# S5 recurrence over chunks: a tree in place of a step-by-step scan

## The chip, the core and the metric

The kernel runs on one core of one Trainium2 chip. TensorE multiplies matrices, VectorE (DVE in the rows) and ScalarE (ACT) work elementwise, GpSimd (POOL) does some elementwise work, memsets and DMA issues, and SyncE (SP) issues most DMAs. The metric is the device time of one execution in microseconds (us), the median of several.

## The reference

One layer of a hybrid decoder for 512 prompt tokens and 8 x 4 sample tokens. The part that matters here is the S5 mixer, a complex recurrence with a diagonal matrix, in 64 groups of 64 states:

```
bu = einsum('btgc,gpc->btgp', u, B)        # complex, as real and imaginary arrays
x_t = lam * x_(t-1) + bu_t                 # per group and state
y = real(einsum('btgp,gcp->btgc', x, C)) + d * u
y = gelu(y);  y = y * sigmoid(y @ glu_w + glu_b)
```

Beside it stand the projections of the normed input (f, q, i, g for eight HGRN2 heads, u for the S5 mixer), the HGRN2 recurrence, an output projection and an MLP with 8192 hidden columns. The final S5 state is an output too.

## The kernel before

All values are float32. To keep the precision, each weight and each activation is split into a high and a low part, and a product is three matmuls (high x high, high x low, low x high). `weights` (L203) loads half of a unit's weights (`wf`, eight 128x128 blocks, three buffers), rounds them on ScalarE to `wh` (L210) and takes the low part `wl = wf - wh` (L211) on the engine that `state["lo"]` names: VectorE at first, GpSimd from gate 1 on, VectorE again after the first S5 outputs. `wh` and `wl` have two buffers. `unit` (L220) makes 128 columns of a projection from two such halves, 96 matmuls over 544 tokens. The units run in this order: u0 to u7, gates g0 to g7, then f, q, i of head 0, of head 1, and so on. A gate (L533) scales the product on VectorE (`gp`), takes a tanh on ScalarE and multiplies on VectorE.

The S5 recurrence is done over chunks of L = 4 tokens. `chunk_inputs(b)` (L563) lets TensorE sum each chunk's inputs (`px`) with maps that `input_maps(b)` (L551) builds on VectorE (`MB`) and transposes (`pw`); ScalarE copies the sums into `XX`, a tile of 128 partitions x 2 (real, imaginary) x 32 pairs of groups x 137 slots, one slot for each chunk: 8 sample slots, a zero slot, then 128 prompt chunks. Two groups of 64 states share the 128 partitions, so one of the 32 `NPR` entries is a pair of groups. Then x_j = lam^4 x_(j-1) + XX_j runs over the 128 prompt slots. In before this is `scan_steps` (L611): for each step j, six VectorE instructions on one slot (two halves of 16 pairs; each one multiply by `coef`, which holds lam^4, and two adds). 13 steps are written behind each of g1 to g7 and behind f, q, i of head 0, and `tc.manual_schedule` fixes the order on VectorE as it is written. Everywhere else a scheduler sets the order of each engine at build time; `tc.high_priority` lifts the weights and the scaling.

After the scan: the final state (`fin`, L641, transposed by TensorE, `pf`), then for each block b of eight pairs' outputs `output_maps(b)` (`CL`, `pk`) and `outputs(b)` (`py`, which reads XX), interleaved with head 1's f, q, i; then the heads, output projection, MLP.

Of the kernel before, what the change touches and what calls it, by code (L numbers as in the profile page):

```python
# [9 lines left out]
F32 = mybir.dt.float32  # L10
# [11 lines left out]
SEQ = 512  # L22
# [18 lines left out]
def trunk_kernel(  # L41
# [66 lines left out]
    with tc.high_priority():  # L108
# [133 lines left out]
    with pool("xs") as xp, tc.manual_schedule(engines={ENG.PE, ENG.Activation, ENG.DVE}):  # L242
# [14 lines left out]
        for k in range(KD + LAG):  # L257
            if k in (1, 8):
                w0[k // 8] = weights(None, 8, P, f"u0_{k}", w_first[k // 8])
            if k < KD:  # L260
                g, e = k // 4, k % 4
# [8 lines left out]
                hi, lo = h_acts[k]  # L270
# [12 lines left out]
            if k >= LAG:  # L283
                j = k - LAG
# [25 lines left out]
    with pool("mk") as mk:  # L310
# [28 lines left out]
    hga = hga_cm.__enter__()  # L339
# [3 lines left out]
    XX = s5.tile([P, 2, NPR, NSLOT], F32, name="XX")  # L343
# [4 lines left out]
    coef = s5.tile([P, 2, 2, NPR], F32, name="coef")  # L348
# [216 lines left out]
    def chunk_inputs(b, WB, ush):  # L565
        for q in range(4):
            i = 4 * b + q
            px = bank(f"px{i}")
            for r in range(2):
                T.matmul(px[:, r * NJ:(r + 1) * NJ], WB[r][:, q, :], ush[:, q, :], start=True, stop=True)  # L570
            pxv = px[:, :2 * NJ].rearrange("p (r j) -> p r j", r=2)
            A.copy(XX[:, :, i, NB + 1:], pxv[:, :, NB:])
            A.copy(WS[:, :, i, :], pxv[:, :, :NB])

    maps = {}
    for n, (mb, ib) in enumerate((([0, 1], []), ([2], [0, 1]), ([3], [2]), ([4], [3]), ([5, 6], [4]), ([7], [5]), ([], [6, 7])), 2):
# [12 lines left out]
    def project(h, after):

        pf = unit(W_IN, FC + P * h, h_acts, f"f{h}")
        f, k, q, v = (hga.tile([P, NT], F32, tag=t, name=f"{t}{h}") for t in "fkqv")
        scaled(f, pf)
        A.activation(f, f, AF.Tanh, scale=0.5)
        V.tensor_scalar(f, f, lbA[:, h:h + 1], lbB[:, h:h + 1], op0=ALU.mult, op1=ALU.add)
        V.tensor_scalar(k, f, -1.0, 1.0, op0=ALU.mult, op1=ALU.add)
        after(0)
        pq = unit(W_IN, QC + P * h, h_acts, f"q{h}")
        scaled(q, pq)
        A.activation(v, q, AF.Tanh, scale=0.5)  # L600
        V.scalar_tensor_tensor(q, v, 1.0, q, op0=ALU.add, op1=ALU.mult)
        after(1)
        pv = unit(W_IN, IC + P * h, h_acts, f"i{h}")
        scaled(v, pv)
        after(2)
        heads[h] = (f, k, q, v)


    s5c_cm = pool("s5c", 2, side="right")
    s5c = s5c_cm.__enter__()  # L610
    HPR = NPR // 2  # L611

    def scan_steps(j0, j1):
        for j in range(j0, min(j1, SEQ // L)):
            part = []
            for g in range(2):
                gs = slice(g * HPR, g * HPR + HPR)
                t = s5c.tile([P, 2, 2, HPR], F32, tag=f"sc{g}", name=f"sc{g}_{j}")
                part.append((t, XX[:, :, gs, NB + j], XX[:, :, gs, NB + 1 + j], coef[:, :, :, gs]))
            for t, xj, xn, cf in part:  # L620
                V.tensor_tensor(t, cf, xj[:, None].to_broadcast([P, 2, 2, HPR]), op=ALU.mult)
            for t, xj, xn, cf in part:
                V.tensor_tensor(xn, xn, t[:, 0], op=ALU.add)
            for t, xj, xn, cf in part:
                V.tensor_tensor(xn, xn, t[:, 1, ::-1, :], op=ALU.add)

    STEPS = 13
    state["lo"] = G
    with tc.manual_schedule(engines={mybir.EngineType.DVE}):
        for k in range(1, 8):  # L630
            gate(k, hga)
            scan_steps(STEPS * (k - 1), STEPS * k)
        project(0, lambda j: scan_steps(STEPS * (7 + j), SEQ // L if j == 2 else STEPS * (8 + j)))
    for a in range(2):
        t = s5c.tile([P, 2, NPR, NB], F32, tag="yn", name=f"scs{a}")
        V.tensor_tensor(t, coef[:, a, :, :, None].to_broadcast([P, 2, NPR, NB]), XX[:, :, :, 0:NB], op=ALU.mult)
# [268 lines left out]
    for k in range(8):  # L905
# [5 lines left out]
        o = tmp.tile([P, NT], F32, tag="ta", name=f"ob{k}")  # L911
# [22 lines left out]
    def x1k(m):  # L934
        return x1[m // 8][:, m % 8, :]
# [74 lines left out]
    for j in range(8):  # L1010
        ps = pair(w_out[0], WA, 2 * P * j, [(ob[0][:, k, :], ob[1][:, k, :]) for k in range(8)], f"ob{j}")
        q = tmp.tile([P, 4, HB], F32, tag="q4", name=f"hq{j}", bufs=1)
        for e in range(2):
            m = 2 * j + e
# [212 lines left out]
    with tc.manual_schedule(engines={ENG.PE, ENG.Activation, ENG.DVE}):  # L1227
# [6 lines left out]
        for s, (job, i) in enumerate(slots):  # L1234
            n, up = s // 7, isinstance(job, Up)
# [136 lines left out]
```

## Time and profile before

| | |
|---|---|
| median of 3 runs | 2544.5 us (2540.7 to 2556.04) |
| profiled execution | 2541.74 us, its span 2540.0 us |
| TensorE busy | 2382.3 us (94%) |
| VectorE busy | 1901.9 us (75%) |
| ScalarE busy | 975.1 us (38%) |
| GpSimd busy | 323.7 us (13%) |
| mean granted TensorE clock | 0.974 |

The span runs from the first to the last instruction. The S5 stretch that the change touches lies between 95 and 455 us. Busy shares are means over stages with different limits; the windows by stage show more. [...]

### The profile page before, as it was taken

How to read it: one execution, taken by the hardware profiler on the slowest of the kernel's cores; microseconds unless marked ns; L12 is line 12 of the kernel's file. 1: busy time of each engine (PE TensorE's matmuls, PEld its weight loads, DVE VectorE, ACT ScalarE, POOL GpSimd, SP SyncE). 2: the span in 40 equal slices, each digit the busy share in tenths (PEclk: the TensorE clock that was granted, in tenths of full speed). 3: DMA queues.
4: the chain of work that ended last, by engine and by line, in shares of the span. 5: the costliest groups of instructions: out<-in, count | busy, mean ns of one | idle time of the engine just before them, and what ended most of it. 6: DMA issues, size and time to landing. Idle time of an engine off the chain costs nothing.

```text
span 2540.0 us, 44792 instructions
## 1 busy us (share of the span) xinstructions
PE 2382.3 (94%) x18386; PEld 2334.1 (92%) x18386; DVE 1901.9 (75%) x3224; ACT 975.1 (38%) x1474; POOL 323.7 (13%) x388
## 2 busy tenths in 40 slices
PE   7899768899999889979999999999899999999997
PEld 7898768799999789979999999999899999999996
DVE  6939985656666634678888888888688888888865
ACT  4241117322221312555555555555333333333344
POOL 0013312211121000210011111110310111011000
PEclk9999889999999999989999999999999999999998
DMA  7332214433233532335555555555964664566354
GB/s 234 94 111 80 85 49 142 149 105 90 77 91 90 181 121 87 126 108 182 188 186 192 192 192 192 189 188 175 339 234 148 223 223 159 164 223 205 100 157 130
DMA packets 303501, 393.88 MB, mean 155 GB/s; under 512 B 14680, under 2 KB 231008, under 8 KB 303104
## 3 DMA queue, kind: packets, MB, share of 16 engines
q1 hardware_dynamic: 265776, 251.49, 32.5%
q0 software_dynamic: 33952, 135.94, 15.0%
q10 hardware_dynamic: 3568, 3.58, 0.5%
q8 instruction: 145, 2.38, 0.4%
q14 instruction: 60, 0.49, 0.1%
HBM read 302.39 MB, written 88.57 MB: 154 GB/s over the span
## 4 chain that ended last, share of the span: by engine, by line
PE 41%; issue 18%; DMA 3%; DVE 2%; POOL 2%; ACT 1%; POOLq 0%; ACTq 0%; SPq 0%; DVEq 0%
PE x_dn L1086 13%; PE y_dn L1086 6%; PE ps_oa L218 4%; PE ps_l L1325 4%; PE ps_ob L218 4%; PE x_up L1086 4%; PE z_dn L1086 3%; POOL ac_d L1143 2%; PE y_up L1086 2%; DMA raw_dn<-in_mlp_down_dram 2%; PE z_up L1086 1%; PE ps_l L218 1%; DVE s_dn L1059 0%; PE pl L1303 0%; DMA wf_oa<-in_w_out_dram 0%
## 5 line engine op out<-in xcount | busy, mean ns | idle before, releaser
L1086 PE MATMUL x_up<-hb,wh_up 128*128 128x272 f32 x2048 | 397.6, 292 | 24.4 <-ACT wh_up L1075 14.7
L1086 PEld LDWEIGHTS x_up<-hb,wh_up 128*128 128x128 f32 x2048 | 325.5, 191 | 30.2 <-issue 15.2
L1086 PE MATMUL x_dn<-ring,wh_dn 128*128 128x272 f32 x1792 | 344.4, 290 | 9.2 <-issue 8.2
L1086 PE MATMUL x_up<-hb,wl_up 128*128 128x272 f32 x1024 | 298.8, 292 | 0.4 <-DVE wl_up L1079 0.4
L1086 PEld LDWEIGHTS x_dn<-ring,wh_dn 128*128 128x128 f32 x1792 | 283.1, 189 | 10.8 <-issue 10.8
L1086 PE MATMUL x_dn<-ring,wl_dn 128*128 128x272 f32 x896 | 260.1, 290 | 0.0
L1075 ACT CAST wh_up<-s_up 128x1024 fp32r<-128x1024 f32 x128 | 134.8, 1053 | 212.1 <-PE x_up L1086 117.8
L1075 ACT CAST wh_dn<-s_dn 128x1024 fp32r<-128x1024 f32 x112 | 118.0, 1053 | 239.3 <-PE x_dn L1086 109.4
L1086 PE MATMUL y_up<-hb,wh_up 128*128 128x272 f32 x1024 | 196.1, 289 | 0.0
L1086 PEld LDWEIGHTS x_up<-hb,wl_up 128*128 128x128 f32 x1024 | 194.8, 190 | 0.8 <-DVE wl_up L1079 0.8
L1086 PE MATMUL y_dn<-ring,wh_dn 128*128 128x272 f32 x896 | 171.6, 289 | 0.0
L1086 PEld LDWEIGHTS x_dn<-ring,wl_dn 128*128 128x128 f32 x896 | 169.5, 189 | 0.0
L1086 PEld LDWEIGHTS y_up<-hb,wh_up 128*128 128x128 f32 x1024 | 161.0, 188 | 0.0
L1079 DVE TENSOR_TENSOR wl_up<-s_up,wh_up 128x1024 fp32r<-128x1024 f32 x128 | 156.0, 1219 | 1.2 <-ACT wh_up L1075 1.1
L1075 ACT CAST wh_dn<-raw_dn 128x1024 fp32r<-128x1024 f32 x84 | 88.5, 1054 | 165.3 <-PE x_dn L1086 109.3
L1086 PE MATMUL y_up<-hb,wl_up 128*128 128x272 f32 x512 | 148.3, 290 | 0.0
L1075 ACT CAST wh_up<-raw_up 128x1024 fp32r<-128x1024 f32 x96 | 101.1, 1053 | 113.1 <-PE x_up L1086 57.8
L1079 DVE TENSOR_TENSOR wl_dn<-s_dn,wh_dn 128x1024 fp32r<-128x1024 f32 x112 | 136.8, 1222 | 7.3 <-ACT wh_dn L1075 5.9
L1086 PEld LDWEIGHTS y_dn<-ring,wh_dn 128*128 128x128 f32 x896 | 140.8, 188 | 0.0
L1174 POOL DMA_DIRECT2D ring<-ac_d x98 | 73.1, 750 | 464.7 <-PE x_dn L1086 401.0
L1086 PE MATMUL y_dn<-ring,wl_dn 128*128 128x272 f32 x448 | 129.6, 289 | 0.0
L1079 DVE TENSOR_TENSOR wl_up<-raw_up,wh_up 128x1024 fp32r<-128x1024 f32 x96 | 117.0, 1219 | 4.7 <-ACT wh_up L1075 4.7
(445 smaller groups left out, 5992.6 us busy)
## 6 DMA issues: line engine op xcount, KB each, us to landing
raw_up<-in_mlp_up_dram SPq DMA_DIRECT2D x64, 1024.0 KB, 5.9
raw_dn<-in_mlp_down_dram SPq DMA_DIRECT2D x56, 1024.0 KB, 5.9
ring<-ac_d POOLq DMA_DIRECT2D x98, 544.0 KB, 12.0
wf_dl<-in_mlp_down_dram SPq DMA_DIRECT2D x16, 1024.0 KB, 5.8
ac_d<-h_up POOLq DMA_DIRECT2D x28, 544.0 KB, 3.0
ac_d<-l_up POOLq DMA_DIRECT2D x28, 544.0 KB, 4.2
ac_d<-h_up POOLq DMA_DIRECT2D x28, 408.0 KB, 4.0
ac_d<-l_up POOLq DMA_DIRECT2D x28, 408.0 KB, 4.0
```

The lines of the kernel that those rows point to most:

```text
L218: T.matmul(ps[:, h, :HB], w, x[:, h * HB:(h + 1) * HB], start=first and j == 0, stop=last and j == 2)
L1075: A.copy(wh, sums[i])
L1079: V.tensor_tensor(wl, sums[i], wh.bitcast(F32), op=ALU.subtract)
L1086: T.matmul(out, w[:, k, :], x[:, k, :], start=start and k == 0 and j == 0, stop=k == nk - 1 and j == 2, skip_group_check=True)
L1143: G.dma_start(ac_d[self.u, :, r, k0:k0 + n, :].bitcast(F32), t.bitcast(F32))
L1174: G.dma_start(t[:, 4 * r:4 * r + 4, :].bitcast(F32), ac_d[4 * c:4 * c + 4, :, r, KIND[i], :].rearrange("q p n -> p q n").bitcast(F32))
L1325: T.matmul(ps[:, e, :HB], w[:, k - k0, es], last[x][h][:, k, :], start=k == 0 and j == 0, stop=k == 7 and j == 2)
```

## The change

The scan is replaced by a tree over the 128 prompt slots, in place in `XX`. A level with distance s = 2^lg adds lam^(4s) times slot k-s to slot k, for every 2s-th k: levels 0 to 6 going up, then 5 to 0 going down. Powers lam^(4s) for s = 1 to 64 are computed once (`pw4`). Levels 0 to 2 of the up sweep and 2 to 0 of the down sweep are done for 8 pairs at a time (four groups), the middle levels for all 32. A level is four VectorE instructions: two multiplies into `tr` (real and imaginary factor), two adds into XX. The up sweep of a group is written behind its chunk inputs, among the u units; the middle behind g0; the down sweep of one group behind each of g1, g3, g5, g7. `state["lo"]` stays VectorE, so all low parts are there. The manual schedule of that stretch goes.

```diff
+    pw4 = s5p.tile([P, 7, 2, 2, NPR], F32, name="pw4")
+    V.tensor_copy(pw4[:, 0], coef)
+    for s in range(6):
+        a, b = pw4[:, s, 0, 0, :], pw4[:, s, 1, 0, :]
+        t0 = s5f.tile([P, NPR], F32, tag="pwa", name=f"pwa{s}")
+        t1 = s5f.tile([P, NPR], F32, tag="pwb", name=f"pwb{s}")
+        V.tensor_tensor(t0, a, a, op=ALU.mult)
+        V.tensor_tensor(t1, b, b, op=ALU.mult)
+        for r in range(2):
+            V.tensor_tensor(pw4[:, s + 1, 0, r, :], t0, t1, op=ALU.subtract)
+        V.scalar_tensor_tensor(pw4[:, s + 1, 1, 0, :], a, 2.0, b, op0=ALU.mult, op1=ALU.mult)
+        V.scalar_tensor_tensor(pw4[:, s + 1, 1, 1, :], a, -2.0, b, op0=ALU.mult, op1=ALU.mult)
+
+    def tree_level(pl, gs, lg, down, name):
+        s = 1 << lg
+        k0 = (3 if down else 2) * s - 1
+        n = len(range(k0, NJ - NB, 2 * s))
+        ng = gs.stop - gs.start
+        o = NB + 1 + k0
+        xk = XX[:, :, gs, o:o + 2 * s * (n - 1) + 1:2 * s]
+        xs = XX[:, :, gs, o - s:o - s + 2 * s * (n - 1) + 1:2 * s]
+        t = [pl.tile([P, 2, ng, n], F32, tag=f"tr{a}", name=f"tr{a}_{name}", bufs=1) for a in range(2)]
+        for a in range(2):
+            V.tensor_tensor(t[a], pw4[:, lg, a, :, gs, None].to_broadcast([P, 2, ng, n]), xs, op=ALU.mult)
+        V.tensor_tensor(xk, xk, t[0], op=ALU.add)
+        V.tensor_tensor(xk, xk, t[1][:, ::-1], op=ALU.add)
...
         for b in ib:
             chunk_inputs(b, *maps.pop(b))
+            if b % 2:
+                tree_up(s5f, b // 2)
...
+    tree_middle(s5t)
+    for k in range(1, 8):
+        gate(k, hga)
+        if k % 2:
+            tree_down(s5t, k // 2)
...
-    def scan_steps(j0, j1):
-        for j in range(j0, min(j1, SEQ // L)):
...
-            for t, xj, xn, cf in part:
-                V.tensor_tensor(t, cf, xj[:, None].to_broadcast([P, 2, 2, HPR]), op=ALU.mult)
-            for t, xj, xn, cf in part:
-                V.tensor_tensor(xn, xn, t[:, 0], op=ALU.add)
-            for t, xj, xn, cf in part:
-                V.tensor_tensor(xn, xn, t[:, 1, ::-1, :], op=ALU.add)
-
-    STEPS = 13
-    state["lo"] = G
-    with tc.manual_schedule(engines={mybir.EngineType.DVE}):
-        for k in range(1, 8):
-            gate(k, hga)
-            scan_steps(STEPS * (k - 1), STEPS * k)
-        project(0, lambda j: scan_steps(STEPS * (7 + j), SEQ // L if j == 2 else STEPS * (8 + j)))
+    project(0, lambda j: None)
```

Where instructions stand now. First VectorE among the u units, ahead of u7 (`cm_mb` and `MB` build the input maps, `wl_u` is a low part, `ut` the scaled unit). Before:

```order
L211 TENSOR_TENSOR wl_u_0_1684<-wf_u_0_1681,wh_u_0_1683 128x1024
L524 TENSOR_TENSOR ut_1625<-ps_u_1516,rb_145 128x4x68 x2
L211 TENSOR_TENSOR wl_u_8_1738<-wf_u_8_1735,wh_u_8_1737 128x1024
L361 TENSOR_TENSOR MB_989<-cm_mb 64x4x16x4 x2
L363 TENSOR_TENSOR MB_989<-cm_mb 64x4x16x4 x2
L211 TENSOR_TENSOR wl_u_0_1879<-wf_u_0_1876,wh_u_0_1878 128x1024
```

Of the change (`tr_u_0`, `tr_u_1` are levels 0 and 1 of an up sweep):

```order
L602 TENSOR_TENSOR tr_u_0_1751<-pw_996,XX 128x1024
L602 TENSOR_TENSOR tr_u_0_1752<-pw_996,XX 128x1024
L603 TENSOR_TENSOR XX<-XX,tr_u_0_1751 128x2x8x64
L361 TENSOR_TENSOR MB_992<-cm_mb 64x4x16x4
L604 TENSOR_TENSOR XX<-XX,tr_u_0_1752 128x2x8x64
L361 TENSOR_TENSOR MB_992<-cm_mb 64x4x16x4
L211 TENSOR_TENSOR wl_u_0_1968<-wf_u_0_1965,wh_u_0_1967 128x1024
L602 TENSOR_TENSOR tr_u_1_1757<-pw_996,XX 128x512
L602 TENSOR_TENSOR tr_u_1_1758<-pw_996,XX 128x512
L603 TENSOR_TENSOR XX<-XX,tr_u_1_1757 128x2x8x32
L363 TENSOR_TENSOR MB_992<-cm_mb 64x4x16x4
L604 TENSOR_TENSOR XX<-XX,tr_u_1_1758 128x2x8x32
```

The two halves of a block's map stood together ahead of u7's low part; now two levels of an up sweep lie between and around them, and the second half stands behind the low part.

Second VectorE in the gates, at the scaling of one gate (`gp`). Before:

```order
L621 TENSOR_TENSOR sc_25_2630<-coef,XX 128x64
L621 TENSOR_TENSOR sc_25_2631<-coef,XX 128x64
L623 TENSOR_TENSOR XX<-XX,sc_25_2630 128x2x16
L623 TENSOR_TENSOR XX<-XX,sc_25_2631 128x2x16
L625 TENSOR_TENSOR XX<-XX,sc_25_2630 128x2x16
L625 TENSOR_TENSOR XX<-XX,sc_25_2631 128x2x16
L531 TENSOR_TENSOR gp_2747<-ps_g_2638,rb_145 128x544
L539 SCALAR_TENSOR_TENSOR gp_2747<-gth_2749,gp_2747 128x544
L621 TENSOR_TENSOR sc_26_2753<-coef,XX 128x64
```

Of the change (`tr_d_2`, `tr_d_1`, `tr_d_0` are the levels of a down sweep):

```order
L531 TENSOR_TENSOR gp_2855<-ps_g_2746,rb_145 128x544
L211 TENSOR_TENSOR wl_g_8_2919<-wf_g_8_2916,wh_g_8_2918 128x1024
L539 SCALAR_TENSOR_TENSOR gp_2855<-gth_2857,gp_2855 128x544
L604 TENSOR_TENSOR XX<-XX,tr_d_2_2977 128x2x8x15
L602 TENSOR_TENSOR tr_d_1_2982<-pw_996,XX 128x496
L602 TENSOR_TENSOR tr_d_1_2983<-pw_996,XX 128x496
L603 TENSOR_TENSOR XX<-XX,tr_d_1_2982 128x2x8x31
L604 TENSOR_TENSOR XX<-XX,tr_d_1_2983 128x2x8x31
L602 TENSOR_TENSOR tr_d_0_2988<-pw_996,XX 128x1008
L602 TENSOR_TENSOR tr_d_0_2989<-pw_996,XX 128x1008
L211 TENSOR_TENSOR wl_g_0_2998<-wf_g_0_2995,wh_g_0_2997 128x1024
L603 TENSOR_TENSOR XX<-XX,tr_d_0_2988 128x2x8x63
```

The 13 scan steps of a gate are gone; one down sweep of eight pairs stands around the scaling of each of gates 2 to 5, and the gate's low parts, formerly on GpSimd, stand inside it.

Third TensorE around the transpose of the final state (`pf`). Before it stands inside head 1's ps_f, 71 matmuls into the unit:

```order
L218 MATMUL ps_f_4505<-h_142,wh_f_8_4562 128x272 x2
L218 MATMUL ps_f_4505<-h_144,wh_f_8_4562 128x272
L642 MATMUL pf_4375<-ident,fin_4376 32x128
L218 MATMUL ps_f_4505<-h_144,wh_f_8_4562 128x272
L218 MATMUL ps_f_4505<-h_142,wl_f_8_4563 128x272 x2
L642 MATMUL pf_4382<-ident,fin_4383 32x128
```

Of the change:

```order
L218 MATMUL ps_i_3476<-h_142,wl_i_8_3534 128x272 x2
L676 MATMUL pf_3592<-ident,fin_3593 32x128
L218 MATMUL ps_f_3722<-h_141,wh_f_0_3725 128x272 x2
L218 MATMUL ps_f_3722<-h_143,wh_f_0_3725 128x272 x2
L218 MATMUL ps_f_3722<-h_141,wl_f_0_3726 128x272 x2
L218 MATMUL ps_f_3722<-h_141,wh_f_0_3725 128x272
L676 MATMUL pf_3599<-ident,fin_3600 32x128
```

It now stands between head 0's last unit and head 1's first.

## Rows read from the trace of the kernel before

**Rows 1.** Windows: us, busy us (instructions) per engine, granted clock, DMA share, GB/s.
```profile
core 0: us, PE busy (x) PEld busy (x) DVE busy (x) ACT busy (x) POOL busy (x), PEclk, DMA share, GB/s
99.35:166.60 67.25, 64.13 (x512) 62.34 (x511) 44.40 (x81) 24.69 (x66) 0.00 (x0) 1.00 0.38 107
344.90:358.40 13.50, 12.16 (x75) 11.62 (x75) 13.50 (x64) 1.99 (x2) 4.82 (x2) 0.76 0.28 80
358.40:372.00 13.60, 0.02 (x1) 0.02 (x2) 13.49 (x84) 0.00 (x0) 0.00 (x0) 0.62 0.02 3
372.00:380.00 8.00, 7.99 (x51) 7.54 (x52) 3.90 (x9) 2.82 (x8) 0.00 (x0) 0.80 0.29 84
380.00:454.00 74.00, 64.60 (x491) 61.91 (x491) 42.85 (x75) 52.75 (x117) 20.05 (x37) 0.95 0.51 145
217.00:341.00 124.00, 101.03 (x701) 97.76 (x699) 118.91 (x550) 17.90 (x21) 33.64 (x14) 0.89 0.25 74
```

**Rows 2.** TensorE timeline: start, us, instruction xcount [idle before <- what ended it].
```profile
340.53 0.41 PE L218 MATMUL ps_i<-h,wl_i 128*128 128x272 f32 x2
344.94 1.28 PE L218 MATMUL ps_f<-h,wh_f 128*128 128x272 f32 x4 [4.00 <-DVE sc L621]
347.46 0.82 PE L218 MATMUL ps_f<-h,wl_f 128*128 128x272 f32 x2 [1.24 <-POOL wl_f L211]
...
371.98 0.40 PE L642 MATMUL pf<-ident,fin 128*32 128x128 f32 x1 [13.64 <-DVE fin L641]
```

**Rows 3.** VectorE groups, 196 to 372 us: xcount | busy us, mean ns | idle before.
```profile
L621 DVE TENSOR_TENSOR sc<-coef,XX 128x64 f32<-128x64 f32 x256 | 64.1, 292 | 0.0
L623 DVE TENSOR_TENSOR XX<-XX,sc 128x32 f32<-128x32 f32 x256 | 62.7, 290 | 0.0
L625 DVE TENSOR_TENSOR XX<-XX,sc 128x32 f32<-128x32 f32 x256 | 59.2, 276 | 0.0
```

**Rows 4.** VectorE timeline, four scan steps.
```profile
208.82 0.49 DVE L621 TENSOR_TENSOR sc<-coef,XX 128x64 f32<-128x64 f32 x2
209.22 0.34 DVE L623 TENSOR_TENSOR XX<-XX,sc 128x32 f32<-128x32 f32 x2
209.47 2.55 DVE L625 TENSOR_TENSOR XX<-XX,sc 128x32 f32<-128x32 f32 x2
211.95 0.46 DVE L621 TENSOR_TENSOR sc<-coef,XX 128x64 f32<-128x64 f32 x2
...
212.83 0.47 DVE L621 TENSOR_TENSOR sc<-coef,XX 128x64 f32<-128x64 f32 x2
...
213.72 0.48 DVE L621 TENSOR_TENSOR sc<-coef,XX 128x64 f32<-128x64 f32 x2
```

**Rows 5.** GpSimd timeline (one row), and its groups from 170 to 372 us.
```profile
209.45 2.39 POOL L211 TENSOR_TENSOR wl_g<-wf_g,wh_g 128x1024 fp32r<-128x1024 f32 x1 [3.56 <-ACT wh_g L210]
...
L211 POOL TENSOR_TENSOR wl_g<-wf_g,wh_g 128x1024 fp32r<-128x1024 f32 x14 | 33.9, 2430 | 168.9 <-ACT wh_g L210 165.3 <-DMA wf_g<-in_w_in_dram 3.6
L211 POOL TENSOR_TENSOR wl_f<-wf_f,wh_f 128x1024 fp32r<-128x1024 f32 x4 | 9.6, 2428 | 26.7 <-ACT wh_f L210 26.7
L211 POOL TENSOR_TENSOR wl_i<-wf_i,wh_i 128x1024 fp32r<-128x1024 f32 x2 | 4.9, 2453 | 13.2 <-ACT wh_i L210 13.2
L211 POOL TENSOR_TENSOR wl_q<-wf_q,wh_q 128x1024 fp32r<-128x1024 f32 x2 | 4.8, 2398 | 13.1 <-ACT wh_q L210 13.1
```

**Rows 6.** VectorE groups, 60 to 200 us, dense operands.
```profile
L211 DVE TENSOR_TENSOR wl_u<-wf_u,wh_u 128x1024 fp32r<-128x1024 f32 x10 | 12.2, 1222 | 4.8 <-ACT wh_u L210 4.7
L356 DVE TENSOR_TENSOR cm_mb<-LP,bb 128x256 f32<-128x256 f32 x8 | 3.4, 427 | 0.2
L636 DVE TENSOR_TENSOR scs<-coef,XX 128x512 f32<-128x512 f32 x2 | 1.3, 678 | 0.0
```

**Rows 7.** VectorE, strided: groups at 476 to 487 us; single lines (min/median/max ns).
```profile
L762 DVE TENSOR_TENSOR f<-f 128x272 f32<-128x272 f32 x2 | 0.9, 434 | 0.0
L755 DVE TENSOR_TENSOR X<-q,f 128x272 f32<-128x272 f32 x2 | 0.8, 421 | 0.0
...
L912 DVE SCALAR_TENSOR_TENSOR ob<-z,yr x8: 1119/1136/1151, 841.4 to 889.6; 128x544 f32<-128x544 f32 x8
L524 DVE TENSOR_TENSOR ut<-ps_u,rb x16: 618/648/733, 56.4 to 164.8; 128x272 f32<-128x272 f32 x16
```

**Rows 8.** Scan lines: min/median/max ns, first and last start.
```profile
L621 DVE TENSOR_TENSOR sc<-coef,XX x256: 260/274/2443, 200.4 to 370.9; 128x64 f32<-128x64 f32 x128
L623 DVE TENSOR_TENSOR XX<-XX,sc x256: 201/215/2425, 200.8 to 371.2; 128x32 f32<-128x32 f32 x128
```

**Rows 9.** VectorE timeline, small instructions.
```profile
73.39 0.18 DVE L357 TENSOR_TENSOR cm_lp<-LP 128x32 f32<-128x32 f32 x1
73.49 0.18 DVE L358 TENSOR_TENSOR cm_lp<-LP 128x32 f32<-128x32 f32 x1
```

**Rows 10.** Gate lines on VectorE: min/median/max ns.
```profile
L531 DVE TENSOR_TENSOR gp<-ps_g,rb x8: 709/716/725, 179.2 to 306.2; 128x544 f32<-128x544 f32 x8
L539 DVE SCALAR_TENSOR_TENSOR gp<-gth,gp x8: 725/726/1662, 182.2 to 307.7; 128x544 f32<-128x544 f32 x8
```

**Rows 11.** TensorE timeline: end of gate 0, last chunk inputs, gate 1.
```profile
176.47 0.41 PE L218 MATMUL ps_g<-h,wl_g 128*128 128x272 f32 x2
...
178.96 2.02 PE L570 MATMUL px<-ush,WB 128*128 128x136 f32 x16
182.31 2.12 PE L570 MATMUL px<-ush,WB 128*128 128x136 f32 x16 [1.34 <-ACT WS L573]
184.19 0.76 PE L218 MATMUL ps_g<-h,wh_g 128*128 128x272 f32 x4
```

More of the change, by code (lines that the diff above doesn't have):

```diff
@@ L544, in trunk_kernel @@
     s5_poles()
+    s5p_cm = pool("s5p", side="right")
+    s5p = s5p_cm.__enter__()
     s5f_cm = pool("s5f", 2, side="right")
@@ L573, in chunk_inputs, with tree_up, tree_middle, tree_down @@
             A.copy(WS[:, :, i, :], pxv[:, :, :NB])
+    pw4 = s5p.tile([P, 7, 2, 2, NPR], F32, name="pw4")
[23 more added lines that the diff above has]
+        V.tensor_tensor(xk, xk, t[1][:, ::-1], op=ALU.add)
+    def tree_up(pl, g):
+        for lg in range(3):
+            tree_level(pl, slice(8 * g, 8 * g + 8), lg, False, f"u{g}_{lg}")
+    def tree_middle(pl):
+        for lg in (3, 4, 5, 6):
+            tree_level(pl, slice(0, NPR), lg, False, f"m{lg}")
+        for lg in (5, 4, 3):
+            tree_level(pl, slice(0, NPR), lg, True, f"n{lg}")
+    def tree_down(pl, g):
+        for lg in (2, 1, 0):
+            tree_level(pl, slice(8 * g, 8 * g + 8), lg, True, f"d{g}_{lg}")
     maps = {}
@@ L606, in project @@
         heads[h] = (f, k, q, v)
+    s5t_cm = pool("s5t", side="right")
+    s5t = s5t_cm.__enter__()
+    tree_middle(s5t)
[3 more added lines that the diff above has]
+            tree_down(s5t, k // 2)
+    s5t_cm.__exit__(None, None, None)
+    s5p_cm.__exit__(None, None, None)
     s5c_cm = pool("s5c", 2, side="right")
     s5c = s5c_cm.__enter__()
-    HPR = NPR // 2
-    def scan_steps(j0, j1):
-        for j in range(j0, min(j1, SEQ // L)):
[L615 to L619, printed above, removed]
-            for t, xj, xn, cf in part:
-                V.tensor_tensor(t, cf, xj[:, None].to_broadcast([P, 2, 2, HPR]), op=ALU.mult)
-            for t, xj, xn, cf in part:
-                V.tensor_tensor(xn, xn, t[:, 0], op=ALU.add)
-            for t, xj, xn, cf in part:
-                V.tensor_tensor(xn, xn, t[:, 1, ::-1, :], op=ALU.add)
-    STEPS = 13
-    state["lo"] = G
-    with tc.manual_schedule(engines={mybir.EngineType.DVE}):
-        for k in range(1, 8):
-            gate(k, hga)
-            scan_steps(STEPS * (k - 1), STEPS * k)
-        project(0, lambda j: scan_steps(STEPS * (7 + j), SEQ // L if j == 2 else STEPS * (8 + j)))
+    project(0, lambda j: None)
     for a in range(2):
```

## The prediction

> **What bounds the kernel now.** I read the views from coarse to fine: stage windows, the TensorE timeline, the VectorE groups, single VectorE and GpSimd rows. The windows [rows 1] show a whole that is bound by TensorE (the page has it busy 94% of the span) with one hole: from 217 to 341 us VectorE is busy 118.91 of 124.00 us while TensorE is busy 101.03 and its granted clock is 0.89; from 358.4 to 372 TensorE does nothing. In the TensorE timeline [rows 2] the last projection of head 0 (ps_i) ends at 340.94; head 1's first (ps_f) then waits 4.00 us, waits again 1.24 us, runs, and stops for 13.64 us until `fin` is copied, which needs the last scan step. So VectorE sets the end of this stretch, and the scan is what it does: 768 instructions in three groups of 256, 186.0 us summed [rows 3].
>
> Why does the scan take so long? Steps 0.88 and 0.89 us apart (211.95, 212.83, 213.72) are undisturbed [rows 4], and 128 of them would want 114 us; they take from 200.4 to 371.7 [rows 8]. The step from 208.82 to 211.95 takes 3.13 us: two adds that take 0.34 elsewhere take 2.55 there, in the very time in which GpSimd computes a low part (209.45, 2.39 us) [rows 4, 5]. GpSimd does 22 low parts (14+4+2+2) of 2.4 us [rows 5]; a scan instruction that meets one stands until it is done.
>
> **The change, part by part.**
> *Removed:* 768 scan instructions and the 22 GpSimd low parts with the stalls that they cause.
>
> *Low parts on VectorE:* 1.22 us each [rows 6], two for each unit, so about half of what one takes from VectorE today.
>
> *Tree, dense price.* 1024 elements cost 1.222 us and 256 cost 0.427 [rows 6]: 0.15 us plus 1.04 ns an element. A multiplicand repeated along the inner axis and a source read in short runs cost nothing extra: scs, 512 elements, 0.678 [rows 6].
>
> *Tree, strided price.* Level lg touches every 2^(lg+1)-th slot of XX. At distance 2 (8 bytes), the 272-element ops of the heads' first levels take 0.421, and in place 0.434 [rows 7], the dense price. At distance 4 (16 bytes), `ob`, 544 elements, takes 1.136 us and `ut`, 272 elements, 0.648 [rows 7]: (1.136-0.15)/544 and (0.648-0.15)/272 are both 1.8 ns an element. The scan's own reads and adds at 548 bytes give 1.9 to 2.0 [rows 8]: (0.274-0.15)/64, (0.215-0.15)/32. I take 1.04 ns for level 0 and 1.85 ns for all others, in the multiply that reads and the add that writes alike. Bounds: 1.04 everywhere below, 1.85 everywhere above.
>
> [...]
>
> *Tree, sum.* Every level has four instructions. Up, for a group: 1024 elements dense 4.9 us, 512 strided 4.4, 256 strided 2.5; 11.8, four groups 47. Middle: 28 instructions, 1664 elements x 4 strided: 16.5. Down, for a group: 240, 496 strided and 1008 dense: 2.4+4.3+4.8 = 11.5, four groups 46. Together 109 us. The powers are 37 tiny instructions; 128x32 ones take 0.18 and can start 0.10 apart [rows 9], so between 3.7 and 6.7 us; 4.8, since half of them depend on the one before.
>
> *The VectorE queue.* It becomes one long queue: the order shows up sweeps between the input maps and low parts, and and around the scaling of gates 2 to 5 a down sweep each with a gate's two low parts inside it. From 99.35 (first map) to the low part of gate 7's second half:
> work already there up to 166.60, 44.4 of 67.25 us [rows 1]; powers 4.8; tree 109; 14 low parts 17.1; seven scalings at 0.716 and six gate products at 0.726 [rows 10], 9.4; scs 1.4. Sum 186, that is 99.4+186 = 285.5. Twice the queue must wait for ScalarE's copies of the last chunk inputs into XX (up sweeps 2 and 3), about 2.5 us each as an estimate from the 5.2 us that pass from the first px matmul of that batch to the next gate [rows 11]. So 291 us.
>
> *What TensorE does then.* A unit of 96 matmuls takes 11.95 us: 20 in 2.49 us from 176.47 to 178.96 [rows 11]. Unstalled, ten units from 184.19 would end at 303.7. With the queue at 291 for gate 7's second half, that half ends at 297; the S5 output maps ahead of f0's low part (about 6 us) cost about 1.5; three units 35.9; ps_i ends at 334 instead of 340.94: **7 us gained**. Queued behind the tree on the way: the maps of block 6 (their second half stands behind two up-sweep levels), for which TensorE and u7 wait several us, and every first-half low part, behind 5 to 6 us of down sweep. These waits are inside the 291, not on top of it.
>
> *After head 0.* The tree is over some 50 us before head 1 starts, so `fin` is early: the 4.00, 1.24 and 13.64 us go [rows 2]. [...] **23 us gained**. The S5 outputs follow as before, with 64.60 of 74.00 us busy [rows 1]; I leave that stretch as it is.
>
> *At no cost:* the GpSimd memsets of CL now wait for the tree's end (their space was the tree's); the first pk needs them 45 us later; without that cover it would cost their few us. Weight loads: three buffers, freed now by VectorE's low parts; a tile is used 18 us after its load is issued at the earliest, so late frees of 2 to 3 us stay hidden. No DMA is added.
>
> Sum: 7+23 = 30 us off the profiled execution's 2541.7 (span 2540.0 and 1.7 around it), 2511.7. That execution lies 2.8 below the median of the three runs (2544.5), so I give 2514.
>
> **Rivals.**
> *A. Strides are cheap, TensorE bounds.* 30.7 thousand elements x 0.81 ns = 25 us leave the queue; ps_i ends at 309, near the 303.7 of TensorE alone. 2514-25 = 2489. For it: the 8-byte rows. Against: four rows at 16 bytes and more.
> *B. No change: level 0 pays too.* (1024+1008) x 16 elements x 0.81 ns = 26 us onto the queue; 2540. For it: XX's rows are 137 elements long, an odd count, and no row shows a read or an add on it at distance 2. Against: 0.421 and 0.434 at distance 2 in other tiles [rows 7].
> *C. Slower.* All of the queue's excess reaches TensorE, because the low parts stand in it. 30 us of it undo the gain, 56 us make the kernel 1% slower; that is a tree 50% dearer. One way: in-place adds pay for the read and for the write, half of all 63 thousand elements, another 26 us beside B's: 2566. Against: the scan's adds, in place at 548 bytes, pay once (0.215).
>
> **Chances.** Forecast 0.57, 2500 to 2528 (my idle and dependency estimates); A 0.17; B 0.21; C 0.05. A measurement here tells about 1% (25 us) from no change. Faster by over 1% (under 2519): A and most of the forecast, 0.66. Within 1%: the rest of it and most of B, 0.29. Slower 0.05. Range 2488 to 2539: A's and B's ends; outside lie C and a little of A and B.
>
> **What would show it.** Right: no idle TensorE over 3 us ahead of `fin`; ps_i ending near 334; tree multiplies of 1024 near 1.22 us, of 512 near 1.10, of 256 near 0.62; VectorE over 95% busy from 100 to 285; TensorE waits in gates 2 to 7 at first-half low parts, 2 to 3 us each; no VectorE instruction of 2.4 us there. Wrong: level-1 ops near 0.68 (A), level-0 adds near 2.0 (B), adds dearer than multiplies (C), or new waits after 334 that return the 23 us, such as pk for CL or py for the chunks.

## The result

The changed kernel takes 2513.0 us in the median of four runs (2507.7 to 2517.2), the kernel before 2545.3: a ratio of 0.9866, with a 95% interval from 0.9829 to 0.9903. A second set of runs (below) gave 2517.1 against 2547.5, 0.9878 with 0.986 to 0.9895. So it is faster by 1.2 to 1.3%, 30 to 32 us; the forecast was 2514 in a range of 2488 to 2539. The profiled execution took 2507.7 us, its span 2505.9. One execution of a run below (3391.2 us) and one of the kernel before (6645.3 us) lie far outside all others and are left out of the ratios.

The windows by stage of the changed kernel, with the columns of [rows 1] (the granted clock is a share of full speed, 1.00):

```profile
core 0: us, PE busy (x) PEld busy (x) DVE busy (x) ACT busy (x) POOL busy (x), PEclk, DMA share, GB/s
99.35:166.60 67.25, 57.07 (x439) 54.95 (x439) 66.45 (x144) 21.92 (x60) 0.00 (x0) 0.97 0.32 91
166.60:197.10 30.50, 27.81 (x225) 27.45 (x225) 19.64 (x22) 11.17 (x29) 0.00 (x0) 1.00 0.37 109
197.10:230.00 32.90, 30.76 (x244) 30.34 (x243) 31.68 (x46) 5.59 (x9) 3.18 (x3) 1.00 0.23 69
230.00:291.00 61.00, 50.95 (x374) 49.88 (x374) 60.48 (x69) 13.20 (x21) 0.99 (x2) 0.94 0.32 93
291.00:335.00 44.00, 44.00 (x354) 43.98 (x353) 23.52 (x39) 12.31 (x16) 0.00 (x0) 1.00 0.40 115
```

VectorE is full up to 166.6 (66.45 of 67.25; before it was 44.40), idle for 11 us around g0, full again from 197 to 291, and about half busy after that; TensorE then runs without a gap. Next TensorE's timeline where head 0 ends (the rows that answer to [rows 2]) and one VectorE row, the last low part of the gates (start, us, instruction, count):

```profile
334.34 0.42 PE L218 MATMUL ps_i<-h,wl_i 128*128 128x272 f32 x2
334.60 0.27 PE L676 MATMUL pf<-ident,fin 128*32 128x128 f32 x1
334.62 0.74 PE L218 MATMUL ps_f<-h,wh_f 128*128 128x272 f32 x4
...
289.42 1.22 DVE L211 TENSOR_TENSOR wl_g<-wf_g,wh_g 128x1024 fp32r<-128x1024 f32 x1
```

Head 0 ends at 334.8 where before had 340.94, the waits of 4.00, 1.24 and 13.64 us are gone, and `ps_f` follows at once. TensorE's waits from 99 to 335 us (waiting line, releaser: us in total, times, longest):

```profile
PE ps_g L218 <- DVE wl_g L211: 12.2, 7, 2.4
PE pw L561 <- ACT WS L575: 4.4, 1, 4.4
PE px L572 <- ACT WS L575: 4.0, 2, 2.7
```

And VectorE's groups from 99 to 330 us (count, busy us, mean ns, idle before):

```profile
L602 DVE TENSOR_TENSOR tr_u<-pw,XX 128x1024 f32<-128x1024 f32 x8 | 9.4, 1219 | 3.9 <-ACT XX L574 3.9
L602 DVE TENSOR_TENSOR tr_u<-pw,XX 128x512 f32<-128x512 f32 x8 | 8.4, 1089 | 0.1
L602 DVE TENSOR_TENSOR tr_u<-pw,XX 128x256 f32<-128x256 f32 x8 | 4.8, 641 | 0.1
L603 DVE TENSOR_TENSOR XX<-XX,tr_u 128x1024 f32<-128x1024 f32 x4 | 4.9, 1220 | 0.0
L603 DVE TENSOR_TENSOR XX<-XX,tr_u 128x512 f32<-128x512 f32 x4 | 4.4, 1110 | 0.0
L603 DVE TENSOR_TENSOR XX<-XX,tr_u 128x256 f32<-128x256 f32 x4 | 2.5, 638 | 0.0
```

Level 0 (8 bytes apart) costs 1219 ns for 1024 elements, the price of the dense low parts (1222 [rows 6]), level 1 (16 bytes) 1089 for 512, level 2 (32 bytes) 641 for 256; the in-place adds cost 1220, 1110 and 638. Rivals A (level 1 near 680), B (level 0 near 2000) and C (adds dearer than multiplies) fall by these rows.

### The profile page after: what moved, and what is told of

Read it like the earlier page. It is cut to its first block, busy times and chain, and to the rows that moved or that the text cites. A ratio compares the mean times of both kernels' runs of the same rounds, so it can differ in the third digit from the quotient of the medians.

```text
span 2505.9 us, 44188 instructions
## 1 busy us (share of the span) xinstructions
PE 2371.7 (95%) x18386; PEld 2325.7 (93%) x18386; DVE 1876.8 (75%) x2639; ACT 978.0 (39%) x1474; POOL 270.7 (11%) x366
## 4 chain that ended last, share of the span: by engine, by line
PE 48%; issue 13%; DMA 3%; DVE 2%; POOL 2%; ACT 1%; POOLq 0%; ACTq 0%; SPq 0%; DVEq 0%
PE x_dn L1120 13%; PE x_up L1120 7%; PE y_dn L1120 6%; PE ps_oa L218 4%; PE ps_l L1359 4%; PE ps_ob L218 4%; PE y_up L1120 4%; PE z_dn L1120 3%; DMA raw_dn<-in_mlp_down_dram 2%; PE z_up L1120 2%; POOL ac_d L1177 1%; PE ps_l L218 1%; PE pl L1337 0%; DMA wf_oa<-in_w_out_dram 0%; DVE s_dn L1093 0%
## 5 line engine op out<-in xcount | busy, mean ns | idle before, releaser
L1120 PE MATMUL x_up<-hb,wh_up 128*128 128x272 f32 x2048 | 396.9, 292 | 23.5 <-ACT wh_up L1109 14.7
L1113 DVE TENSOR_TENSOR wl_up<-s_up,wh_up 128x1024 fp32r<-128x1024 f32 x128 | 156.0, 1219 | 1.2 <-ACT wh_up L1109 1.1
L1113 DVE TENSOR_TENSOR wl_dn<-s_dn,wh_dn 128x1024 fp32r<-128x1024 f32 x112 | 136.9, 1222 | 7.3 <-ACT wh_dn L1109 5.9
L1113 DVE TENSOR_TENSOR wl_up<-raw_up,wh_up 128x1024 fp32r<-128x1024 f32 x96 | 117.0, 1219 | 4.7 <-ACT wh_up L1109 4.7
```

Of the source, the lines that this page charges most:

```text
L1113: V.tensor_tensor(wl, sums[i], wh.bitcast(F32), op=ALU.subtract)
L1120: T.matmul(out, w[:, k, :], x[:, k, :], start=start and k == 0 and j == 0, stop=k == nk - 1 and j == 2, skip_group_check=True)
```

## Experiments

Each kernel ran beside the kernel before on the same chip; times are medians, the ratio is to before; the last two columns (us) are read from the profiled execution of each run.

| run | us | ratio (95%) | ps_i of head 0 ends | i of head 1 ends |
|---|---|---|---|---|
| before | 2545 to 2549 | 1 | 340.9 | 448.5 |
| changed | 2513.0 | 0.9866 (0.9829, 0.9903) | 334.8 | 416.9 |
| e1 scan, low parts on VectorE, order freed | 2520.8 | 0.9893 (0.9879, 0.9908) | 331.5 | 424.4 |
| e2 tree, low parts on GpSimd | 2540.1 | 0.9972 (0.9959, 0.9985) | 359.7 | 444.9 |
| e3 unit stride | 2494.0 | 0.9784 (0.9768, 0.98) | 315.3 | 399.1 |
| e4 no tree | 2481.8 | 0.9741 (0.9727, 0.9756) | 306.0 | 388.4 |
| e5 down sweeps written later | 2516.4 | 0.987 (0.9853, 0.9886) | 335.1 | 418.9 |
| e8 all written later | 2509.7 | 0.9846 (0.9832, 0.9861) | 330.3 | 415.1 |
| e9 order by hand | 2507.4 | 0.9848 (0.983, 0.9866) | 319.8 | 413.0 |
| e10 order by hand, lighter | 2504.0 | 0.983 (0.9814, 0.9847) | 321.9 | 410.9 |
| e11 order by hand, mended | 2491.1 | 0.9779 (0.9765, 0.9794) | 308.1 | 392.5 |
| changed, again | 2517.1 | 0.9878 (0.986, 0.9895) | 334.5 | 423.4 |

### The two halves of the change, one at a time

The first run keeps the scan and takes the other half of the change:

```diff
-    state["lo"] = G
-    with tc.manual_schedule(engines={mybir.EngineType.DVE}):
-        for k in range(1, 8):
+    for k in range(1, 8):
```

> The kernel before with one half of the change: all low parts on VectorE and no fixed order there, the scan kept. My theory (VectorE's work sets fin, and both halves count): 128 undisturbed steps of 0.885 us are 114 us, 20 low parts of 1.22 us 24, the scalings and products 14, from 200 us on: fin at about 352 us where before had 371.7, so some 18 to 20 us faster than before, 2524 us; no VectorE instruction of 2.4 us is left. Rival one (the stalls by GpSimd were all of it, the tree adds nothing): as fast as the changed kernel, 2513. Rival two (the tree is all of it, low parts on VectorE cost there what they save): 2540 to 2546.

The second keeps the tree and gives the low parts back to GpSimd:

```diff
     tree_middle(s5t)
+    state["lo"] = G
     for k in range(1, 8):
```

> The changed kernel with the low parts of g1 to head 1 back on GpSimd, the tree kept. My theory (a VectorE instruction that meets a GpSimd low part stands until it is done, so 2.4 us are lost instead of 1.22 spent): 14 low parts up to g7 add 14 x 1.2 = 17 us to VectorE's queue, some of it where VectorE waits anyway: ps_i about 10 us later than 334.8, 2524 us in all (2518 to 2531), tree instructions of up to 2.4 us beside low parts. Rival (GpSimd takes the low parts off VectorE for nothing): 17 us less on the queue, 2497.

The first gave 2520.8, my number within 4 us. But its edit changes two things: the low parts go to VectorE, and the fixed order goes too (the second line of the diff), which the expectation left out. In the line of the scan's multiplies (min/median/max ns, first and last start) no instruction is stretched any more (293 at most), where before had up to 2443 [rows 8]; the next row is TensorE's wait for `fin`, 5.51 us where before had 13.64. Then the windows from 184.2 us to `fin`, of before and of this run, and VectorE's wait for a gate's tanh there (us in total, times, longest), again of before and of this run:

```profile
L621 DVE TENSOR_TENSOR sc<-coef,XX x256: 253/276/293, 185.4 to 345.7; 128x64 f32<-128x64 f32 x128
...
346.73 0.40 PE L640 MATMUL pf<-ident,fin 128*32 128x128 f32 x1 [5.51 <-DVE fin L639]
...
184.20:371.80 187.60, 145.99 (x1038) 142.18 (x1036) 180.09 (x812) 31.34 (x46) 50.64 (x24) 0.88 0.25 74
184.20:346.53 162.33, 133.85 (x1029) 129.74 (x1029) 160.63 (x834) 34.59 (x58) 0.53 (x1) 0.99 0.30 86
...
DVE gp L539 <- ACT gth L538: 5.1, 7, 0.7
DVE gp L539 <- ACT gth L538: 1.0, 1, 1.0
```

`fin` is 25.3 us earlier. Of these, 19.5 are busy time of VectorE (180.09 to 160.63): the three scan groups fall from 186.0 us [rows 3] to 150.4, against 19 low parts of 1.22 us that are added; the rest is in other instructions, such as gate products, which had stood too (up to 1662 ns for one [rows 10]), and in overlaps. The other 5.8 are idle time (7.5 to 1.7), most of it the waits for the tanh that the fixed order kept. So by these two traces some three quarters of this run's gain come from the low parts and one quarter from the freed order; no run moves the low parts and keeps the order, so this split is not shown by an experiment.

The second missed: 2540.1, outside my 2518 to 2531, and only 7 us under before. VectorE's and GpSimd's rows in one gate of it, the same two VectorE instructions in the changed kernel, and the windows from g0's scaling to g7's, of this run and of the changed kernel:

```profile
269.19 5.43 DVE L602 TENSOR_TENSOR tr_d<-pw,XX 128x240 f32<-128x240 f32 x2
...
268.11 6.06 POOL L211 TENSOR_TENSOR wl_g<-wf_g,wh_g 128x1024 fp32r<-128x1024 f32 x2 [12.88 <-ACT wh_g L210]
...
258.41 1.19 DVE L602 TENSOR_TENSOR tr_d<-pw,XX 128x240 f32<-128x240 f32 x2
...
196.50:323.80 127.30, 98.45 (x690) 96.30 (x691) 115.92 (x129) 26.09 (x50) 40.49 (x18) 0.87 0.25 74
192.60:302.90 110.30, 95.47 (x724) 93.98 (x725) 106.46 (x143) 27.77 (x50) 4.17 (x5) 0.97 0.31 90
```

Two instructions that together take 1.19 us in the changed kernel take 5.43 beside two low parts: a low part costs VectorE 2.1 us of standing, instead of the 1.13 from start to start that it costs there when it does it itself. From g0's scaling to g7's it is 127.3 us where the changed kernel has 110.3 (starts 196.5 and 323.8; 192.6 and 302.9). These 17 us are the number that I had worked out and then cut to 10, but they are made of other parts: VectorE is busy 9.5 us longer (115.92 against 106.46) and idle 7.5 us longer (11.4 against 3.8), mostly waiting for chunk inputs (3.8), for the tanh (2.6) and, at g7, for TensorE (3.7). So it does wait there, and more than in the changed kernel. Another 4 us were late before g0, where two low parts of g1 stretch two pairs of up-sweep multiplies to 4.30 and 3.30 us (1.09 and 0.64 us for each single one in the changed kernel), and 4 more because TensorE no longer ran ahead of VectorE at g7 (its last matmul of g7 ended at 298.7 in the changed kernel, 4.2 before the scaling); together 25 us, 359.7 against 334.8.

The standing shows on both sides: GpSimd's low parts of the gates last 2738 ns in the median in this run (2362 to 3362) where those of f0, q0, i0 and f1, with the tree over, last 2386 to 2399. No row names what the two engines hold each other up at.

So low parts and order without the tree bring 26.5 us (2547.3 to 2520.8), the tree with the low parts on GpSimd 7.3, and the whole change 30 to 32: over four fifths of the gain come without the tree. What the tree adds, 4 to 8 us (2520.8 against 2517.1 and 2513.0), is no more than the 10 us by which executions of the changed kernel differ. In the traces head 0 even ends earlier without it (331.5 against 334.8); what the tree then saves is the wait for `fin`.

### What the tree still costs, and what its strides cost

The next run lets each level touch neighbouring slots, so that its sums are no longer the recurrence's; the one behind it leaves the tree out.

```diff
-        xk = XX[:, :, gs, o:o + 2 * s * (n - 1) + 1:2 * s]
-        xs = XX[:, :, gs, o - s:o - s + 2 * s * (n - 1) + 1:2 * s]
+        xk = XX[:, :, gs, o:o + n]
+        xs = XX[:, :, gs, o - s:o - s + n]
```

> The changed kernel with every tree level reading and writing neighbouring slots in place of every 2s-th: same instructions and element counts, wrong sums, so the output is not the reference's. My theory (an element at 16 bytes or more apart costs 1.85 ns, next to each other 1.04): the 512-element instructions fall from 1.09 to 0.68 us, 256 from 0.64 to 0.43, 25 us leave VectorE's queue, and TensorE is bound by its own matmuls in the gates: ps_i near 312, 2490 us (2485 to 2497). Rival (the cost is one of the instruction's shape with its three free dimensions, not of the distance): 2513, no change.

```diff
     def tree_level(pl, gs, lg, down, name):
+        return
```

> The changed kernel without any tree level: the recurrence over chunks is left out, so the output is not the reference's; the low parts stay on VectorE. It is the floor that TensorE sets. My theory: the last chunk inputs end at 184 as before instead of 197, ten units of 11.95 us follow without a wait, ps_i ends at 304 where the changed kernel has 334.8: 31 us faster than it, 2482 us. Rival (part of TensorE's waits there come from its weights or from ScalarE, not from VectorE): 2490 to 2505.

Both came as expected, 2494.0 and 2481.8. Groups and windows of the first, and a window of the second:

```profile
L602 DVE TENSOR_TENSOR tr_u<-pw,XX 128x512 f32<-128x512 f32 x8 | 5.2, 687 | 0.1
L602 DVE TENSOR_TENSOR tr_u<-pw,XX 128x256 f32<-128x256 f32 x8 | 3.0, 411 | 0.1
...
187.00:273.00 86.00, 84.67 (x678) 84.47 (x678) 81.21 (x123) 25.16 (x47) 4.17 (x5) 1.00 0.36 104
...
187.00:250.00 63.00, 63.00 (x505) 63.00 (x504) 28.59 (x42) 17.20 (x24) 0.54 (x2) 1.00 0.36 105
```

With the same shapes and counts, 512 elements fall from 1089 to 687 ns: the price is that of the distance. With the strides gone TensorE is busy 84.67 of 86.00 us in the gates, and without the tree all the time; the 31 to 35 us between the changed kernel and 2481.8 are what TensorE loses to the tree, 29 of them ahead of head 0's end (334.8 against 306.0).

### Can the tree be hidden?

From 99 to 306 us VectorE is idle for 106 of 207 us in the run without a tree, and the tree's instructions occupy 103 (110 summed, some 0.1 us of each beside the next). (An expectation below has 125 and 92 for these two; the traces don't bear that out.) The first two tries only write it at other places.

```diff
-        if k % 2:
-            tree_down(s5t, k // 2)
+        if k in (2, 4, 6):
+            tree_down(s5t, (2, 4, 6).index(k))
+    project(0, lambda j: tree_down(s5t, 3 + (1,).index(j)) if j in (1,) else None)
```

> The changed kernel with the four down sweeps written behind g2, g4, g6 and q0 in place of g1, g3, g5 and g7 (each group's outputs need its sweep only after head 0). My theory (VectorE's queue is the bound up to g7's last low part at 291, and has 20 of 44 us free from there to the end of head 0): about one down sweep, 9 us, and its low-part waits leave the gates: gates 1 to 7 lose 6 to 10 us, ps_i ends at 325 to 329, 2504 us (2499 to 2509); VectorE's busy share in the gates falls under 95%. Rival (the low-part waits come from the order of low parts and sweeps, not from the amount of work): 2513.

The next writes up sweeps behind u6, g0, g1 and g2, the middle behind g3, down sweeps behind g4, g6, f0 and q0:

```diff
-            if b % 2:
-                tree_up(s5f, b // 2)
+        if n in (6, 8):
+            tree_up(s5p, n // 2 - 3)
...
     for k in range(1, 8):
         gate(k, hga)
-        if k % 2:
-            tree_down(s5t, k // 2)
+        if k < 3:
+            tree_up(s5p, k + 1)
+        if k == 3:
+            tree_middle(s5p)
+        if k in (4, 6):
+            tree_down(s5p, k // 2 - 2)
+    project(0, lambda j: tree_down(s5p, 2 + j) if j < 2 else None)
```

> The changed kernel with the same tree written later: up sweeps behind u6, g0, g1 and g2, the middle behind g3, down sweeps behind g4, g6, f0 and q0. My theory: from 99 to 306 us VectorE has 125 us without other work when TensorE never waits (the run without a tree), the tree takes 92; spread evenly it costs TensorE little: the u stage ends at 186 to 190 instead of 197, ps_i at 307 to 313, 2486 us (2482 to 2494), near the 2482 without any tree. Rival one (any tree work between the low parts stalls them, wherever it is): 2500 to 2513. Rival two (head 1's outputs now wait for the later sweeps): ps_i early, but a wait of over 5 us before the first py and 2500.

Both missed. In the first the sweeps start at 230.0, 244.4, 259.0 and 273.5 (229.5, 243.9, 258.4 and 273.0 in the changed kernel): the edit moved nothing, which fits a scheduler that orders by what is ready. In the second the u stage is relieved as meant (g1's matmuls start at 186.6 instead of 197.1), but again every gate gets a whole sweep, a gate takes 14.7 us, and 6 of the 10 us are lost again by head 0's end. Windows of the two (columns as above):

```profile
230.00:291.00 61.00, 52.45 (x385) 51.30 (x385) 60.45 (x68) 12.57 (x19) 1.00 (x2) 0.94 0.32 92
...
250.00:310.00 60.00, 50.91 (x373) 49.84 (x373) 59.31 (x66) 12.31 (x17) 0.99 (x2) 0.94 0.32 93
```

So the order was written by hand (`make` loads and rounds one half of a unit's weights and takes its low part, `tree_for` takes that many us of single instructions from the tree, `late` is the last gate's product, `cols` are g1 to g7 and head 0's f, q and i):

```diff
+    with tc.manual_schedule(engines={mybir.EngineType.DVE}):
+        make(0, 0)
...
+        for n, (name, c0) in enumerate(cols):
+            tree_for(1.2)
+            make(n, 8)
+            if late:
+                late()
+            tree_for(4.2)
...
+                if k0 == 0:
+                    make(n + 1, 0)
+                    tree_for(2.9)
...
+            ps = unit(W_IN, c0, h_acts, name, hook)
...
+            scaled(dst, ps)
```

> The changed kernel's tree with VectorE's order from g1 to head 0 written out by hand: up sweeps of groups 0 and 1 behind u6 and g0, and the rest as a stream of single instructions of which about 8.3 us stand in each of ten units, with the next unit's first low part in its middle and the second right behind the scaling. In the two runs that only wrote the sweeps at later places the sweeps started at the same times as in the changed kernel (230, 244 us) or filled every gate with a whole sweep: the scheduler pulls forward what is ready. My theory (what TensorE loses in a gate is VectorE's 11 us of tree beside 3.6 us of other work in a unit of 12): with 8.3 us of tree a unit takes 12.0 to 12.4 us instead of 14.6, ps_i ends at 308 to 314, 2488 us (2484 to 2496). Rival (a low part is late because the rounding on ScalarE is, wherever the tree stands): units of 14 us, 2505.

The lighter one has 3.6 and 2.6 in place of 4.2 and 2.9:

> As the run before it in this call, with about 7.4 us of tree a unit, so that the last group's sweep ends behind i0. My theory: units of 12.0 us, ps_i at 307 to 310, 2486 us; within 4 us of the run before. Rival (the sweeps that end later hold up the space for the output maps and so head 1): 5 us or more slower than it, with a wait before the first pk.

They took 2507.4 and 2504.0, not 2488 and 2486. The units did what was expected (in the lighter run TensorE is busy 60.00 of 60.00 us from 250 to 310), but two waits stood elsewhere: g1's low part behind the second up sweep, in both (the row is the lighter run's), and in the first the second copy of the final state behind the output maps (the last row). The lighter run's trace lost time in two more places: it is 4.7 us behind the first's at the first input map already (TensorE there at 112.16 against 107.43), for a reason that was not taken apart, and it waits 4.94 us at a `pk` in head 1 (last section).

```profile
250.00:310.00 60.00, 60.00 (x482) 60.00 (x481) 58.89 (x70) 13.68 (x16) 0.00 (x0) 1.00 0.35 104
205.85 0.82 PE L218 MATMUL ps_g<-h,wl_g 128*128 128x272 f32 x2 [7.49 <-DVE wl_g L211]
...
326.91 0.40 PE L748 MATMUL pf<-ident,fin 128*32 128x128 f32 x1 [5.22 <-DVE fin L747]
```

The last version mends them (`at` is the unit behind which the up sweep of group `g` stands):

```diff
+        if n == 8:
+            make(0, 0)
+            make(0, 8)
-        for at, g in ((6, 0), (8, 1)):
+        for at, g in ((6, 0), (7, 1)):
...
-        fin = s5c.tile([P, NPR], F32, name=f"fin{r}", tag="un")
+        fin = s5c.tile([P, NPR], F32, name=f"fin{r}", bufs=1)
```

> As e10 with three places mended that its trace and e9's show: the second up sweep now stands behind u7, in the 15 us in which VectorE has little to do during g0 (in e10 g1's low part stood behind it and TensorE waited 7.5 us); about 7.8 us of tree a unit; and the copies and the outgoing tiles of the final state have space of their own (in e9 the second copy stood behind the output maps and TensorE waited 5.2 us). My theory (each of these waits costs the whole kernel its length, since TensorE bounds everything else): ps_i at 307 to 312, head 1's units as in the changed kernel, 2490 us (2485 to 2497). Rival (the output maps, which now start 15 us later than in the changed kernel, take it back in head 1): 2500 or more, with waits before pk of over 3 us.

> The changed kernel once more, on the chip of the run before, for a comparison of the two on one chip: 2508 to 2518 us.

It took 2491.1 us, and the changed kernel on the same chip 2517.1: 26 us less (22 less than its first set) with as many VectorE instructions, 2639 in both. The window from g1 to the end of head 0:

```profile
187.00:310.00 123.00, 122.08 (x974) 121.61 (x973) 118.87 (x149) 33.13 (x53) 4.17 (x5) 1.00 0.36 106
```

TensorE is busy 122.08 of 123 us at a granted clock of 1.00 while VectorE is busy 118.87. Head 0 ends at 308.1, 2 us behind the run without any tree. This version beats both kernels.

## Why the prediction was right

*What bounds.* VectorE's queue, as said: with the tree gone from it, the kernel gains 31 to 35 us. Of the signs, TensorE's waits at low parts came, but smaller (seven, 12.2 us in all, at most 2.4), and no VectorE instruction of 2.4 us is left there. Two did not hold: VectorE is busy 93% from 100 to 285, not over 95%, and TensorE is idle once for 4.4 us ahead of `fin`, at a map's transpose at 141.9 (`pw`).

*Prices.* 1.22, 1.10 and 0.62 us were forecast for multiplies of 1024, 512 and 256; 1.219, 1.089 and 0.641 measured. The tree's instructions sum to 110.3 us, forecast 109; the powers take 3.8, forecast 4.8. The price is the dense one at 8 bytes (1.219 us for 1024) and higher at 16 (1.089 for 512, against 0.687 side by side in the run with unit strides), as the rows at 8 and 16 bytes [rows 7] had it.

*The queue.* Forecast until 291, measured 290.6, but by two errors that cancel, which is luck. The 186 us of work were 178.3 busy, since many instructions overlap the next by some 0.1 us (the low part at 289.42 takes 1.22, the next instruction starts at 290.55); the 5 us of waiting were 13.4, most of it around g0, where VectorE waits for `ps_u`, the gate's rounding and the chunk inputs.

*TensorE until head 0's end.* Forecast 334, measured 334.8, and here too by another route. The forecast let TensorE wait for the low part of g7's second half and then for f0's. It waits for neither: its last wait is for g7's first half, and the second half's low part is ready at 290.6 and first used at 292.25.

```profile
285.36 0.52 PE L218 MATMUL ps_g<-h,wl_g 128*128 128x272 f32 x2 [2.26 <-DVE wl_g L211]
...
292.25 0.41 PE L218 MATMUL ps_g<-h,wl_g 128*128 128x272 f32 x2
```

From there g7 ends at 298.7 (forecast 297), f0 follows without the 1.5 us that were put down for the output maps, and three units take 36.1 (forecast 35.9). That the sum comes out within 1 us is luck. The shape of the stretch I did not give: the u stage ends 12.9 us later than before (197.11 against 184.19), behind the up sweeps, and the ten units take 137.7 instead of 156.8, so 19 us come back.

*After head 0.* Forecast 23 us. From head 0's end to that of head 1's i it is 82.1 us instead of 107.6, 25.5 less; in the second profile of the changed kernel 88.9, 18.7 less. The windows of that stretch, of before and of the two profiles, and of its first 20 us in the first profile:

```profile
340.94:448.50 107.56, 79.27 (x568) 75.59 (x569) 73.29 (x240) 55.86 (x122) 24.13 (x37) 0.87 0.39 111
334.80:416.90 82.10, 73.06 (x568) 70.10 (x567) 46.88 (x83) 55.29 (x122) 19.33 (x35) 0.98 0.48 137
334.50:423.40 88.90, 75.93 (x569) 73.05 (x568) 46.68 (x82) 55.13 (x122) 19.34 (x35) 0.94 0.46 129
...
334.80:355.00 20.20, 19.00 (x152) 18.16 (x151) 5.28 (x10) 14.41 (x34) 0.00 (x0) 1.00 0.32 95
```

The idle 18.9 us of [rows 2] are gone in both, and the granted clock is 0.98 and 0.94 where it was 0.87. The rest of the 23 us, about 4.5, stands for matmuls at a low granted clock, a term that no run shows by itself. What the runs showed in its place: the 126 matmuls of the windows at 0.76 and 0.80 [rows 1] are busy 20.15 us, 0.160 each, and the 152 of the last window above 19.00 at 1.00, 0.125 each; at that price 126 would take 15.8, as an estimate 4.4 less. What keeps the second profile behind the first is a wait at `pk` for CL, one of the forecast's signs of being wrong (last section).

*What was not in it.* It summed both halves into one queue. That the scan's 114 undisturbed us and the tree's 109 are nearly equal stood in it, but not the conclusion that the low parts, without the tree, would bring most of the gain. The freed order, worth some 6 us of idle time by the trace of the first run, is not in it either.

*Open.* Why the u stage's order puts up sweeps between the maps and the low parts is the scheduler's choice and was not taken apart. Strides that cost nothing in a layout with right sums were not tried.

## What to carry to other kernels

Take the cheaper half of a change by itself first: here it brought over four fifths of the gain. Look at what a second engine does to the one that bounds: moving small work off VectorE to GpSimd cost more than doing it there, 2.1 us of standing for 1.13 of work. Where an engine bounds, what is added to its queue can arrive in full and bring waits of its own: with the low parts on GpSimd, between the scalings of g0 and g7, 9.5 us more of busy time came with 7.5 us more of waiting. And where a scheduler fills by readiness, moving a call in the source need not move the work; read the starts before trusting the edit, and write the order out when a few instructions too many in each unit are the loss.

## What the runs showed of the hardware

The same kernel differs by some 10 us from one execution to the next (2507.7 to 2517.2). The two profiles of the changed kernel (2507.7 and 2518.0 us) agree within 0.3 us at the ends of head 0's i and of head 1's q (386.4 and 386.2); head 1's i ends at 416.9 and 423.4. The difference is one chain of waits. Rows of the first profile, then the same of the second: GpSimd's issue that loads a block's S5 outputs back from DRAM (`yn<-y_d`, behind the stores `y_d<-ysb`), the first VectorE instruction on it, TensorE's `pk` that waits for CL, and a window of 29 matmuls from there:

```profile
380.51 0.56 POOL L735 DMA_DIRECT2D yn<-y_d  x1 [3.64 <-DMA y_d<-ysb]
383.91 0.78 DVE L742 SCALAR_TENSOR_TENSOR yn<-un,prm,yn 128x544 f32<-128x544 f32 x1
390.39 0.46 PE L713 MATMUL pk<-CL,Bm 128*128 128x128 f32 x2 [0.39 <-DVE CL L361]
390.39:394.20 3.81, 3.50 (x29) 3.33 (x29) 3.15 (x7) 0.90 (x2) 2.22 (x5) 1.00 1.03 266
...
383.94 0.56 POOL L735 DMA_DIRECT2D yn<-y_d  x1 [5.63 <-DMA y_d<-ysb]
388.22 0.79 DVE L742 SCALAR_TENSOR_TENSOR yn<-un,prm,yn 128x544 f32<-128x544 f32 x1 [3.60 <-issue]
394.64 0.77 PE L713 MATMUL pk<-CL,Bm 128*128 128x128 f32 x2 [4.79 <-DVE CL L361]
394.64:400.79 6.15, 6.15 (x29) 6.15 (x29) 3.15 (x7) 1.79 (x4) 1.98 (x4) 0.51 0.91 257
```

In the second, GpSimd waits 5.63 us for the store where it was 3.64 and issues the load 3.4 us later; VectorE's next instruction in order starts 4.3 us later, after standing for 3.60 (the profile names no releaser; the load is what it reads), and q's scaling, a low part and CL stand behind it. So TensorE waits 4.79 us at `pk` instead of 0.39, and then runs 29 matmuls at a granted clock of 0.51, in 6.15 us instead of 3.81 at 1.00. The two make up the 6.6 us. The written order's lighter run shows the same chain: 4.65 us for the store, 4.33 for the load, 4.94 at `pk`. Why the store takes longer in one execution than in another is open; no run here controls it.
